# RWKV-7 inverse from blocks of 16 with pairs joined on TensorE, and sigmoids written with the hyperbolic tangent

## The chip, the cores and the metric

The kernel runs on one core of a Trainium2 chip, in one launch. The metric is the time of that launch on the device in microseconds (us). PE is TensorE, PEld its weight load, DVE is VectorE, ACT is ScalarE, POOL is GpSimd, and SP is SyncE, which issues all of this kernel's DMAs.

## The reference, cut to what matters

A decoder trunk of two layers works on 1024 tokens of width 1024: layer 0 is a latent attention (MLA) mixer, layer 1 an RWKV-7 mixer. Both have a memory cross-attention beside them and a gated output projection. The change lies in layer 1:

```python
def rwkv7_mixer(u_shift, mu, w0, w2, a0, a2, k_k, k_a, r_k, gn_w, gn_b):
    ...
    w = -jax.nn.softplus(-(w0 + jnp.tanh(wd) @ w2)) - 0.5
    decay = jnp.exp(-jnp.exp(w))
    a = jax.nn.sigmoid(a0 + ad @ a2)
    ...
    y = rwkv7_scan(r, decay, k, v, kk, a)      # 24 heads of 64 channels
def step(state, inp):                          # of rwkv7_scan, once for each token
    sa = einsum('bhvk,bhk->bhv', state, -kk_t)
    state = state * w_t + sa[..., None] * (kk_t * a_t) + v_t[..., None] * k_t
    return state, einsum('bhvk,bhk->bhv', state, r_t)
y = concatenate([mix, mem_out]) * jax.nn.silu(gate)
```

The decay of the reference equals exp(-exp(-0.5) * sigmoid(w0 + tanh(wd) @ w2)), so a sigmoid stands there too. The kernel computes the scan in chunks of 64 tokens. Within a chunk the tokens' feedback through `sa` is a strictly triangular 64x64 matrix A for each head, and the chunk needs the inverse of (I - A).

## The kernel before, in words

All products of weights are done in three passes of float32r (`mm3`, L162 to L164): high times high, high times low, low times high. A weight tile comes by DMA (`wr`, L152), ACT casts it to the high part (`wh`, L153), and in layer 1 DVE makes the low part (`wl`, L155). There are 4 buffers each of `wr`, `wh` and `wl`.

Layer 1 handles 24 items: 12 pairs of heads in each of 2 halves of 512 tokens; an item is 128 channels (2 heads) by 512 tokens (8 chunks), hence 16 systems of 64x64. An item goes through five stages, one in each of five successive steps of a software pipeline: `project` (r, k, v), `prep`, `invert`, `scan`, `norm`. In one step five items are in the works, one in each stage, and `interleave` writes their pieces in turns, with projections, memory heads and output projections as extra pieces. A scheduler then reorders each engine's instructions by its own account of durations and readiness; each engine and the SP queue run their list strictly in order. So an instruction that waits holds up everything behind it on its engine.

`prep` makes decays, keys and A: two low-rank products and sigmoids (`sig`, `a`, L998), three exponentials (L1038 to L1040), and the products masked into `AM` (L1090). It then writes the two diagonal 32x32 blocks of each system to DRAM (`sysd`, 16 DMAs of 8 KB, L1106) and copies the off-diagonal blocks A21 on ACT (L1109).

`invert` reads the blocks back with each one on 4 partitions (`As`, L1121; 32 blocks, 128 partitions), and a unit matrix split over those partitions (`U`, L1133), so that each partition solves for 8 columns. The back substitution is 31 pairs of DVE instructions, a product (`tmp`, L1139) and a sum (`U`, L1143) over up to 76 elements a partition. Eight transposes on PE (L1151) and four ACT copies (L1155) bring the solved blocks to the tile `inv` of 96 partitions (rows 0-31 A21, 32-63 and 64-95 the two inverted diagonal blocks). The off-diagonal block of the 64x64 inverse is U1 * A21 * U2: a DVE transpose (`X1`, in the trace X, L1159), four products on PE (L1174), four ACT copies (`M1`, L1183), four products (L1188), two ACT copies into `XT` (L1191). `XT` is the operand of the first dependent product of each chunk in `scan` (`c<-gm,XT`, L1221). The `scan` goes chunk by chunk between PE and DVE: L1217, `gm` (L1219), L1221, `SAV` (L1222), L1224, `S` (L1236).

On ACT, a table of functions is loaded (ACT_TABLE_LOAD) whenever the next function is not in the one that is active; in layer 1 the sigmoids (L998, and L864 in the gates) take turns with exponentials (L1037 to L1040, L304).

Of the kernel before, what the change touches and what calls it, by code (L numbers as in the profile page):

```python
# [71 lines left out]
class Build:  # L72
# [51 lines left out]


# [653 lines left out]
    def layer1(self, x1, first, second):  # L779

        nc, A, tc = self.nc, self.A, self.tc
        with ExitStack() as st:
# [19 lines left out]

            cen = tl([P, P], F32, "cen")
# [4 lines left out]
            for t in ARs + XTs + [U2]:  # L808
                nc.gpsimd.memset(t[:], 0.0)
# [169 lines left out]
    def prep(self, d, env):  # L979
# [14 lines left out]
        for j, (t, bias) in enumerate(((sig, PW0), (a, PA0))):  # L994
            ps = a_tile()
            mm(ps[:], wh[:, j * P : j * P + P], twa[j][:], start=True, stop=False)
            mm(ps[:], wl[:, j * P : j * P + P], twa[j][:], start=False, stop=True)
            ACT.activation(t[:], ps[:], AF.Sigmoid, bias=self.pc(bias + p))  # L998
# [98 lines left out]

        sysd = self.dram.tile([2, 16, 32, 32], F32, tag=f"sys{p % 2}", name=self.name("sysd"))
        inv = self.g([P, 16, 32], s="inv")
        A21 = inv[0:32]  # L1100
        for b in range(2):
            for i in range(4):
                src = AM[i][32 * b : 32 * b + 32, :, 0:128].rearrange("p c (h t) -> p c h t", h=2)
                dst = sysd[b, 4 * i : 4 * i + 4].rearrange("(c h) r t -> r c h t", h=2)
                for c in range(2):
                    nc.sync.dma_start(dst[:, c], src[:, c, :, 32 * b : 32 * b + 32])  # L1106
        for i in range(4):
            src = AM[i][0:32, :, 0:128].rearrange("p c (h t) -> p c h t", h=2)
            ACT.copy(A21[:, 4 * i : 4 * i + 4, :].rearrange("p (c h) t -> p c h t", h=2), src[:, :, :, 32:64])  # L1109
        d.update(f=f, SAV=SAV, BKT=BKT, AM=AM, bonus=bonus, inv=inv, sysd=sysd)  # L1110

    def invert(self, d, env):

        XT, U2, inv, sysd = (d[x] for x in ("XT", "U2", "inv", "sysd"))
# [5 lines left out]
        As = ip.tile([P, 32, 32], F32, tag="As", name=self.name("As"))  # L1120
        nc.sync.dma_start(  # L1121
            As[:].rearrange("p a b -> p (a b)"),
            sysd[:].rearrange("b s r t -> (b s) (r t)").unsqueeze(1).broadcast_to([32, 4, 1024]),
        )
        U = ip.tile([P, 32, 8], F32, tag="U", name=self.name("U"))
        tmp = ip.tile([P, 32, 8], F32, tag="tmp", name=self.name("tmp"))
        E = V
        if d["hf"] == 1:
            c0 = self.smp.tile([P, P], F32, tag="c0", bufs=2, name=self.name("c0"))
            nc.sync.dma_start(c0[:], self.carry[d["p"]][:])  # L1130
            ACT.activation(c0[:], c0[:], AF.Copy, scale=d["f"][:, 8:9])
            d["c0"] = c0[:]
        nc.sync.dma_start(U[:].rearrange("p a b -> p (a b)"), self.A["cst"][:, CU : CU + 256])  # L1133
        for u in range(31, 0, -1):
            if u % 4 == 0:
                yield
            i0 = u // 4
            n = 8 - i0
            E.tensor_tensor(  # L1139
                out=tmp[:, 0:u, 0:n], in0=As[:, 0:u, u : u + 1].broadcast_to([P, u, n]),  # L1140
                in1=U[:, u : u + 1, i0:8].broadcast_to([P, u, n]), op=ALU.mult,
            )
            E.tensor_tensor(out=U[:, 0:u, i0:8], in0=U[:, 0:u, i0:8], in1=tmp[:, 0:u, 0:n], op=ALU.add)  # L1143
        yield

        Uc = [inv[32:64], inv[64:96]]
        for ih in range(2):
            yield
            ps = b_tile()
            for i in range(4):  # L1150
                nc.tensor.transpose(ps[0:32, i * P : i * P + P], U[:, :, ih * 4 + i], self.ident)  # L1151
            for b in range(2):
                src = ps[0:32, :].rearrange("p (i s c) -> p i s c", i=4, c=4)[:, :, b * 16 : b * 16 + 16, :]
                dst = Uc[b][:, :, ih * 16 : ih * 16 + 16].rearrange("p s (i c) -> p i s c", c=4)
                ACT.copy(dst, src)  # L1155
# [143 lines left out]
def host_constants():  # L1299
# [79 lines left out]
```

## Time and profile before

| | |
|---|---|
| median of 3 runs | 2585.66 us (2582.15 to 2588.03) |
| the profiled execution's own time | 2576.96 us |
| its span, first to last instruction | 2575.1 us |
| mean granted TensorE clock | 0.991 |
| first and last `As` read (L1121) | 1088.2 and 2422.6 us after the span's start |
| DMA packets of the kernel | 165983, 231.46 MB |

The profiled execution is 8.7 us shorter than the median. The stretch from the first to the last `As` read, 1334 us, is called the pipeline stage below: it holds all 24 inversions but the end of the last.

### The profile page before, as it was taken

Reading aid. Unit: us, or ns where it says so; the run is one execution under the profiler, and the core shown is the slowest. Engines: PE = TensorE matmul, PEld = TensorE weight load, DVE = VectorE, ACT = ScalarE, POOL = GpSimd, SP = SyncE. Lnnn points to the kernel's source line nnn. Section 1 sums busy time; section 2 is a strip of 40 time slices with the busy share of each in tenths; the row PEclk is TensorE's granted clock in tenths of the full one; section 3 lists DMA queues with packets and bytes.
Section 4 is the critical chain, followed back from the end, with each engine's and each line's share of the span. In section 5 each row is a group of like instructions: output and inputs, shape, how many; then the busy total and the mean of one; then the engine's idle time right before and its main releaser. Section 6 shows DMA issues by size and latency. Waiting matters only on the chain.

```text
span 2575.1 us, 39906 instructions
## 1 busy us (share of the span) xinstructions
PE 2440.8 (95%) x13298; PEld 2004.1 (78%) x13298; DVE 1897.9 (74%) x5492; ACT 1374.2 (53%) x2971; POOL 367.7 (14%) x416
## 2 busy tenths in 40 slices
PE   7899999999999999999999999999999999999997
PEld 5687778888888788877777777777777777778775
DVE  6755334777777646698888888788888888786975
ACT  5444335555545434565665666666665655654542
POOL 4332222222211330010000000000000010000000
PEclk9999999999999999999999999999999999999998
DMA  4252222111112444422122222322222222232341
GB/s 161 86 172 89 80 82 76 47 59 50 56 60 70 142 158 145 139 79 74 61 65 74 77 74 83 103 78 78 70 77 73 69 85 94 94 99 96 107 146 68
DMA packets 165983, 231.46 MB, mean 90 GB/s; under 512 B 46096, under 2 KB 67984, under 8 KB 165776
## 3 DMA queue, kind: packets, MB, share of 16 engines
q1 hardware_dynamic: 165776, 228.90, 27.1%
q8 instruction: 105, 1.72, 0.3%
q14 instruction: 102, 0.84, 0.1%
HBM read 187.66 MB, written 37.49 MB: 87 GB/s over the span
## 4 chain that ended last, share of the span: by engine, by line
PE 64%; DVE 19%; ACT 5%; issue 5%; DMA 2%; SPq 0%; POOL 0%; POOLq 0%; DVEq 0%; ACTq 0%
PE mm L162 12%; PE mm L164 12%; PE mm L163 12%; PE a L1088 3%; DVE U L1143 2%; DVE tmp L1139 2%; PE pt L726 2%; DVE wl L155 2%; PE po L162 1%; PE po L163 1%; PE c L1221 1%; PE po L164 1%; PE c L1224 1%; DVE u L1019 1%; PE c L1215 1%
## 5 line engine op out<-in xcount | busy, mean ns | idle before, releaser
L153 ACT CAST wh<-wr 128x512 fp32r<-128x512 f32 (+3 forms) x500 | 298.7, 600 | 442.8 <-PE mm L163 362.8
L162 PE MATMUL mm<-xnh,wh 128*128 128x512 f32 x912 | 376.5, 413 | 0.6 <-DVE qml L134 0.4
L164 PE MATMUL mm<-xnh,wl 128*128 128x512 f32 x912 | 370.7, 407 | 1.1 <-DVE wl L155 1.1
L163 PE MATMUL mm<-xnl,wh 128*128 128x512 f32 x912 | 370.0, 406 | 0.0
L155 DVE TENSOR_TENSOR wl<-wr,wh 128x512 fp32r<-128x512 f32 (+2 forms) x352 | 238.5, 679 | 115.8 <-ACT wh L153 84.2
L155 POOL TENSOR_TENSOR wl<-wr,wh 128x512 fp32r<-128x512 f32 (+1 forms) x148 | 186.5, 1264 | 575.9 <-ACT wh L153 445.0
L162 PE MATMUL mm<-yh,wh 128*128 128x512 f32 x492 | 199.7, 406 | 5.9 <-DVE xr L391 5.9
L164 PE MATMUL mm<-yh,wl 128*128 128x512 f32 x492 | 196.3, 399 | 0.2 <-DVE wl L155 0.2
L162 PEld LDWEIGHTS mm<-xnh,wh 128*128 128x128 f32 x912 | 172.7, 190 | 30.4 <-issue 3.3
L164 PEld LDWEIGHTS mm<-xnh,wl 128*128 128x128 f32 x912 | 172.6, 189 | 29.9 <-DVE wl L155 1.3
L163 PE MATMUL mm<-yl,wh 128*128 128x512 f32 x492 | 195.4, 397 | 0.0
L163 PEld LDWEIGHTS mm<-xnl,wh 128*128 128x128 f32 x912 | 173.0, 190 | 26.1 <-issue 0.8
L162 PE MATMUL mm<-xh,wh 128*128 128x512 f32 x416 | 168.1, 405 | 7.7 <-ACT xh L440 7.7
L1235 ACT ACTIVATE sc<-S,f 128x128 f32<-128x128 f32 x168 | 67.4, 401 | 195.3 <-DVE S L1236 184.0
L1143 DVE TENSOR_TENSOR U<-U,tmp 128x60 f32<-128x60 f32 (+24 forms) x744 | 159.7, 215 | 13.5
L163 PE MATMUL mm<-xl,wh 128*128 128x512 f32 x416 | 167.5, 403 | 2.0 <-DVE xl L441 2.0
L164 PE MATMUL mm<-xh,wl 128*128 128x512 f32 x416 | 167.1, 402 | 0.0
L1139 DVE TENSOR_TENSOR tmp<-As,U 128x60 f32<-128x60 f32 (+24 forms) x744 | 157.1, 211 | 13.3 <-DMA U<-in_cst_dram 0.2
L992 POOL TENSOR_TENSOR w2l<-w,w2h 128x256 fp32r<-128x256 f32 x24 | 20.8, 865 | 897.9 <-ACT w2h L991 859.4
L304 ACT ACTIVATE p<-b,sm 128x512 f32<-128x512 f32 (+2 forms) x144 | 83.0, 580 | 117.5 <-DVE sm L301 78.2
L391 DVE TENSOR_TENSOR xr<-mm,xr 128x512 f32<-128x512 f32 x123 | 84.4, 688 | 77.2 <-PE mm L164 76.8
L162 PEld LDWEIGHTS mm<-yh,wh 128*128 128x128 f32 x492 | 92.8, 189 | 24.3 <-DVE xr L391 3.8
(362 smaller groups left out, 6300.0 us busy)
## 6 DMA issues: line engine op xcount, KB each, us to landing
wr<-in_wu_dram SPq DMA_DIRECT2D x292, 256.0 KB, 2.6
wr<-in_wo_dram SPq DMA_DIRECT2D x122, 256.0 KB, 2.6
yr<-y SPq DMA_DIRECT2D x60, 256.0 KB, 3.7
As<-sysd SPq DMA_DIRECT2D x24, 512.0 KB, 4.3
y<-y SPq DMA_DIRECT2D x32, 256.0 KB, 2.0
y<-sg SPq DMA_DIRECT2D x32, 256.0 KB, 2.1
g<-u SPq DMA_DIRECT2D x24, 256.0 KB, 2.5
gt<-g SPq DMA_DIRECT2D x24, 256.0 KB, 2.8
```

The source lines that it names most:

```text
L153: nc.scalar.copy(hi[:, :n], raw[:, :n])
L155: sub(lo[:, :n], raw[:, :n], hi[:, :n].bitcast(F32))
L162: mm(ps, a[0], b[0], start=start, stop=False)
L163: mm(ps, a[0], b[1], start=False, stop=False)
L164: mm(ps, a[1], b[0], start=False, stop=stop)
L304: nc.scalar.activation(p[:, :own], ps[:, :own], AF.Exp, bias=sm[:, 0:1], accum_out=sm[:, 2 + i : 3 + i])
L391: nc.vector.tensor_add(xs[m][:], ps[:], xs[m][:])
L726: nc.tensor.transpose(pt[:, o : o + P], src, self.ident)
L1088: mm(ps[:, j * 256 : j * 256 + 256], BK[c // 4][:, c % 4, :], AR[:, c, :], start=True, stop=True)
L1139: E.tensor_tensor(out=tmp[:, 0:u, 0:n], in0=As[:, 0:u, u : u + 1].broadcast_to([P, u, n]), in1=U[:, u : u + 1, i0:8].broadcast_to([P, u, n ...
L1143: E.tensor_tensor(out=U[:, 0:u, i0:8], in0=U[:, 0:u, i0:8], in1=tmp[:, 0:u, 0:n], op=ALU.add)
L1235: ACT.activation(sc[:], cur, AF.Copy, scale=fc)
```

## The change

It has two parts.

**The inverse.** The systems are written to DRAM whole (`sysd`, 8 DMAs of 64x2x64), and `invert` reads their four diagonal 16x16 blocks with each block on 2 partitions (`As`, 8 DMAs; 64 blocks, 128 partitions), and A21 (1 DMA in place of the four ACT copies). The back substitution is 15 pairs of DVE instructions of 8 to 120 elements a partition. The solved 16x16 blocks go to DRAM twice, as they are (`Wd`, 2 DMAs) and transposed in the row (`WT`, 2 DMAs, after the ACT copy `UT`). From there come the operands of the join (`W1T`; `W2`, in the rows W; and, from `sysd`, `N12`, in the rows N, 2 DMAs), and, in 4 DMAs, the 16x16 diagonal pieces of `inv`. The join of two 16-blocks to one 32-block is W1 * N12 * W2 for 32 pairs: four products on PE of 8 pairs each (new L1178), a mask on DVE (`Tb`, new L1183), four products on PE (new L1190), an ACT copy (`Ws`), a DMA to DRAM (`Wx`, new L1193) and two DMAs back to `inv` (new L1195). The eight transposes and the four copies L1155 are gone. From `inv` on (`X1`, new L1202; new L1217; `M1`, new L1226; new L1231; `XT`, new L1234; scan's new L1264) all is as before. `inv` is one tile for all items in place of a tile of the heap for each.

**The sigmoids.** sigmoid(x) becomes 0.5 * tanh(0.5 x) + 0.5: an ACTIVATE with Tanh and one with Copy, in `prep` (2 for each item) and in the gates (32 in all). The biases w0 and a0 are halved in place once.

```diff
+    def sigmoid(self, out, src, bias=None):
+        ACT.activation(out, src, AF.Tanh, scale=0.5, bias=0.0 if bias is None else bias)
+        ACT.activation(out, out, AF.Copy, scale=0.5, bias=0.5)
...
+            blk = tl([P, P], F32, "blk")
+            nc.sync.dma_start(blk[:], A["cst"][:, CU + P : CU + 256])
+            inv = tl([96, 16, 32], F32, "inv")
+            half = self.prm[:, PW0 : PW0 + 24]
+            nc.vector.tensor_scalar_mul(half, half, 0.5)
...
-                nc.scalar.activation(sg[:], ps[:], AF.Sigmoid)
+                self.sigmoid(sg[:], ps[:])
...
-            ACT.activation(t[:], ps[:], AF.Sigmoid, bias=self.pc(bias + p))
+            self.sigmoid(t[:], ps[:], env["half"][:, bias - PW0 + p : bias - PW0 + p + 1])
...
-        for b in range(2):
-            for i in range(4):
-                ...
-                for c in range(2):
-                    nc.sync.dma_start(dst[:, c], src[:, c, :, 32 * b : 32 * b + 32])
         for i in range(4):
-            ACT.copy(A21[:, 4 * i : 4 * i + 4, :].rearrange("p (c h) t -> p c h t", h=2), src[:, :, :, 32:64])
+            for c in range(2):
+                dst = sysd[4 * i + 2 * c : 4 * i + 2 * c + 2].rearrange("h r t -> r h t")
+                nc.sync.dma_start(dst, AM[i][0:64, c, 0:128].rearrange("p (h t) -> p h t", h=2))
...
-        nc.sync.dma_start(As..., sysd[:]...broadcast_to([32, 4, 1024]))
+        for half in range(2):
+            for i in range(4):
+                q = half * 64 + i % 2 * 32 + i // 2 * 16
+                nc.sync.dma_start(As[q : q + 16], sysd[:, 16 * i : 16 * i + 16, 16 * i : 16 * i + 16])
+        nc.sync.dma_start(A21, sysd[:, 0:32, 32:64].rearrange("s r t -> r s t"))
...
-        for u in range(31, 0, -1):
+        for u in range(15, 0, -1):
...
+        ACT.copy(UT[:].rearrange("p n r -> p r n"), U[:])
+            nc.sync.dma_start(Wd[:]...[:, :, cs], U[64 * half : 64 * half + 64])
+            nc.sync.dma_start(WT[:, cs, :], UT[64 * half : 64 * half + 32])
+        nc.sync.dma_start(W1T[:], WT[:].rearrange("q k m -> k q m"))
...
+        ps = b_tile()
+        for g in range(4):
+            mm(ps[:, g * P : g * P + P], N12[:, 8 * g : 8 * g + 8, :]..., W1T[:, 8 * g : 8 * g + 8, :]..., start=True, stop=True)
+        V.tensor_tensor(out=Tb[:], in0=ps..., in1=env["blk"]..., op=ALU.mult)
+        ps = b_tile()
+        for g in range(4):
+            mm(ps[:, g * 16 : g * 16 + 16], Tb[:, g, :], W2[:, g, :], start=True, stop=True)
+        ACT.copy(Ws[:].rearrange("p g n -> p (g n)"), ps[:, 0:64])
+        nc.sync.dma_start(Wx[:].rearrange("(g e) m n -> (e m) g n", e=8), Ws[:])
+        for j in range(2):
+            nc.sync.dma_start(inv[32 + 32 * j : 48 + 32 * j, :, 16:32], Wx[16 * j : 16 * j + 16]...)
-        for ih in range(2):
-            ...
-                nc.tensor.transpose(ps[0:32, i * P : i * P + P], U[:, :, ih * 4 + i], self.ident)
-            ...
-                ACT.copy(dst, src)
```

**How it stands in the engines' lists.** The scheduler's lists of the two kernels are the same up to the start of layer 1 but for the halving of the biases. The rows below are those of the fifth item (of 24) in the built programs; x4 is four equal rows, and a number behind a name tells buffers apart. First PE before, from the join of the 32-blocks (X is `X1`, the second M is `M1`) to the first product of scan that reads `XT`; the rows between the two pieces are all of one projection, and 22 rows lie between the last L1188 and L1221:

```order
L1174 MATMUL b_14048<-X_3043_14038,inv_13420 128x128 x4
L164 MATMUL mm_14120<-xnh_10265,wl_14110 128x512
L162 MATMUL mm_14120<-xnh_10292,wh_14109 128x512
L163 MATMUL mm_14120<-xnl_10293,wh_14109 128x512
L164 MATMUL mm_14120<-xnh_10292,wl_14110 128x512
L1188 MATMUL b_14058<-U_10130,M_3045_14053 32x128 x4
L162 MATMUL mm_14120<-xnh_10365,wh_14109 128x512
...
L1221 MATMUL c_14195<-gm_14193,XT_10128 128x128
```

PE now, from the new join of the 16-blocks to the same product; the rows left out are 24 of one projection:

```order
L1178 MATMUL b_13930<-W1T_13858,N_3055_13860 128x128 x2
L168 MATMUL mm_14064<-xnh_10474,wh_14059 128x512
L169 MATMUL mm_14064<-xnl_10475,wh_14059 128x512
L170 MATMUL mm_14064<-xnh_10474,wl_14060 128x512
L168 MATMUL mm_14064<-xnh_10519,wh_14059 128x512
L1190 MATMUL b_13962<-W_3056_13863,Tb_13935 128x16 x4
L169 MATMUL mm_14064<-xnl_10520,wh_14059 128x512
...
L1217 MATMUL b_13986<-X_3082_13976,inv 128x128 x4
L1231 MATMUL b_13996<-U_10134,M_3084_13991 32x128 x4
L1264 MATMUL c_14136<-gm_14134,XT_10132 128x128
```

Projection matmuls that stood between the steps of the old join now stand between L1190 and L1217, and none is left between L1217, L1231 and L1264. In 7 of the 24 items (the 1st, 3rd, 4th, 5th, 14th, 17th and 18th) no matmul stands between the last L1231 and L1264, and 0 to 2 between L1217 and L1231; in the other 17 there are 1 to 10 and 4. Before, 4 to 42 stood ahead of the use of `XT` and 4 to 12 between L1174 and L1188. Between L1178 and L1190 there are 4 in 11 items and 7 to 62 in the others; between L1190 and L1217 there are 26 to 38 in every item.

SP before, around the read of the same item's blocks:

```order
L1106 DMA sysd_13419<-AM_13354 32x2x32
L152 DMA wr_13941<-in_wu_dram 128x512
L1121 DMA As_13511<-sysd_13419 128x1x1024
L152 DMA wr_13947<-in_wu_dram 128x512
L1133 DMA U_13513<-in_cst_dram 128x256
L990 DMA w_3169_14635<-in_w2a_dram 128x256
```

SP now, from the read of the join's operands of that item to the loads behind it:

```order
L1159 DMA W1T_13858<-WT_13832 16x32x16
L1162 DMA N_3055_13860<-sysd_13378 16x16x16 x2
L1171 DMA inv<-Wd_13831 16x16x16 x3
L1112 DMA sysd_13937<-AM_13872 64x2x64 x2
L1193 DMA Wx_13833<-Ws_13967 128x4x16
L1139 DMA U_14031<-in_cst_dram 128x128
L158 DMA wr_14611<-in_wu_dram 128x512
L1130 DMA As_14021<-sysd_13937 16x16x16
L1195 DMA inv<-Wx_13833 16x16x16 x2
L1130 DMA As_14021<-sysd_13937 16x16x16 x7
L1131 DMA inv<-sysd_13937 32x16x32
L158 DMA wr_14617<-in_wu_dram 128x512
```

The queue has 361 rows more than before (1708 for 1347), and weight loads (`wr`) now stand behind DMAs that wait for PE's and ACT's part of the join.

More of the change, by code (lines that the diff above doesn't have):

```diff
@@ L807, in layer1 @@
             U2 = tl([P, 4, P], F32, "U2")
-            for t in ARs + XTs + [U2]:
+            for t in ARs + XTs + [U2, inv]:
                 nc.gpsimd.memset(t[:], 0.0)
@@ L1119, in invert @@
         V, G, ACT = nc.vector, nc.gpsimd, nc.scalar
[L1120 to L1127, printed above, removed]
+        As = ip.tile([P, 16, 16], F32, tag="As", name=self.name("As"))
@@ L1131, in invert @@
             ACT.activation(c0[:], c0[:], AF.Copy, scale=d["f"][:, 8:9])
             d["c0"] = c0[:]
-        nc.sync.dma_start(U[:].rearrange("p a b -> p (a b)"), self.A["cst"][:, CU : CU + 256])
-        for u in range(31, 0, -1):
-            if u % 4 == 0:
+        nc.sync.dma_start(U[:].rearrange("p a b -> p (a b)"), self.A["cst"][:, CU : CU + P])
+        for u in range(15, 0, -1):
+            if u % 2 == 0:
                 yield
[L1137 to L1141, printed above, removed]
-            )
-            E.tensor_tensor(out=U[:, 0:u, i0:8], in0=U[:, 0:u, i0:8], in1=tmp[:, 0:u, 0:n], op=ALU.add)
@@ L1144, in invert @@
-        yield
-        Uc = [inv[32:64], inv[64:96]]
-        for ih in range(2):
[L1148 to L1155, printed above, removed]
+            V.tensor_tensor(
+                out=tmp[:, 0:u], in0=As[:, 0:u, u : u + 1].broadcast_to([P, u, 8]),
+                in1=U[:, u : u + 1, :].broadcast_to([P, u, 8]), op=ALU.mult,
+            )
@@ new lines, in invert @@
+            V.tensor_tensor(out=U[:, 0:u], in0=U[:, 0:u], in1=tmp[:, 0:u], op=ALU.add)
+        UT = ip.tile([P, 8, 16], F32, tag="UT", name=self.name("UT"))
+        ACT.copy(UT[:].rearrange("p n r -> p r n"), U[:])
+        dt = lambda shape, n: self.dram.tile(shape, F32, tag=f"{n}{p % 2}", name=self.name(n))
+        Wd, WT, Wx = dt([2, 32, 16, 16], "Wd"), dt([32, 16, 16], "WT"), dt([32, 16, 16], "Wx")
+        for half in range(2):
+            cs = slice(8 * half, 8 * half + 8)
+            nc.sync.dma_start(Wd[:].rearrange("a q r n -> (a q) r n")[:, :, cs], U[64 * half : 64 * half + 64])
+            nc.sync.dma_start(WT[:, cs, :], UT[64 * half : 64 * half + 32])
@@ new lines, in invert @@
+        yield
+        W1T = self.g([16, 32, 16], s="W1T")
+        nc.sync.dma_start(W1T[:], WT[:].rearrange("q k m -> k q m"))
+        N12 = self.g([16, 32, 16], s="N12")
+        for j in range(2):
+            nc.sync.dma_start(
+                N12[:, 16 * j : 16 * j + 16, :],
+                sysd[:, 32 * j : 32 * j + 16, 32 * j + 16 : 32 * j + 32].rearrange("s k n -> k s n"),
+            )
+        W2 = ip.tile([P, 4, 16], F32, tag="W2", name=self.name("W2"))
+        nc.sync.dma_start(W2[:], Wd[1].rearrange("(g e) k n -> (e k) g n", e=8))
@@ new lines, in invert @@
+        for par in range(2):
+            for j in range(2):
+                r0, c0 = 32 + 32 * j + 16 * par, 16 * par
+                nc.sync.dma_start(
+                    inv[r0 : r0 + 16, :, c0 : c0 + 16], Wd[par, 16 * j : 16 * j + 16].rearrange("s r n -> r s n")
+                )
+        yield
+        ps = b_tile()
+        for g in range(4):
+            mm(
+                ps[:, g * P : g * P + P], N12[:, 8 * g : 8 * g + 8, :].rearrange("p q n -> p (q n)"),
+                W1T[:, 8 * g : 8 * g + 8, :].rearrange("p q m -> p (q m)"), start=True, stop=True,
+            )
@@ L1156, in invert @@
+        nc.sync.dma_start(Wx[:].rearrange("(g e) m n -> (e m) g n", e=8), Ws[:])
+        for j in range(2):
+            nc.sync.dma_start(
+                inv[32 + 32 * j : 48 + 32 * j, :, 16:32], Wx[16 * j : 16 * j + 16].rearrange("s r n -> r s n")
+            )
+        Uc = [inv[32:64], inv[64:96]]
         yield
```

33 lines of the change are left out of this document (20 added, 13 removed).

## Prediction

> **What bounds the kernel now.** I read the busy times first, then the pipeline stage alone, then the chain of waits there, then who makes PE wait.
>
> ```profile
> PE 2440.8 (95%) x13298; PEld 2004.1 (78%) x13298; DVE 1897.9 (74%) x5492; ACT 1374.2 (53%) x2971; POOL 367.7 (14%) x416
> ```
> ```profile
> 1088.00:2423.00 1335.00, 1268.78 (x7008) 1024.86 (x7007) 1118.03 (x3781) 807.25 (x1767) 99.26 (x112) 1.00 0.25 81
> ```
> ```profile
> by line: PE mm L162 9.4%; PE mm L164 9.3%; PE mm L163 9.1%; PE a L1088 5.7%; issue 3.6%; DVE U L1143 3.3%; DVE tmp L1139 3.2%; DVE wl L155 2.8%; PE c L1221 2.3%; PE c L1224 2.1%; DVE u L1019 2.0%; PE c L1215 2.0%; DVE L L1027 1.9%; PE y L12
> ```
>
> The second row is the pipeline stage: length, then PE, PEld, DVE, ACT and POOL busy. PE is at 95%, but DVE is at 84%, against 74% over the whole kernel. The third row is the chain of waits in that stage: besides projections, it runs through DVE, and the back substitution alone (U and tmp) holds 6.5%, 87 us of 1335. So PE is the first bound, with DVE close behind it: PE's list is held where a result of DVE or ACT is late.
>
> ```profile
> PEld c L1221 <- DVE gm L1219: 17.4, 30, 1.5
> PEld c L1215 <- DVE S L1236: 11.5, 35, 0.9
> PEld b L1151 <- ACT inv L1155: 11.4, 18, 0.8
> ```
> ```profile
> PEld b L1188 <- ACT M L1183: 10.2, 22, 0.6
> ```
>
> The four rows are waits of the weight loads in the stage (us in total, times, longest): all short, under 2 us, and many. The third goes away with the change.
>
> How much idle time there is to win depends on how PE's busy time is read. By PE's row the stage has 66 us in which PE does nothing, by the weight loads' row 310 us. The Trainium skill (Perfetto Trace Analysis, the note at its head) calls matmul busy time a bad metric, since matmuls are pipelined, and wants the weight loads' share: by that rule the larger figure holds, and a large gain (the third rival) is possible; by PE's row alone it could not pass 66 us. The trace bears the rule out in part: matmuls last 0.41 us in the groups and start every 0.23 us (rows below).
>
> **DVE's part.**
>
> ```profile
> L1143 DVE TENSOR_TENSOR U<-U,tmp 128x60 f32<-128x60 f32 (+24 forms) x713 | 153.3, 215 | 13.3
> L1139 DVE TENSOR_TENSOR tmp<-As,U 128x60 f32<-128x60 f32 (+24 forms) x713 | 150.2, 211 | 13.0 <-DMA U<-in_cst_dram 0.2
> L1090 DVE TENSOR_TENSOR AM<-a,cst 128x512 f32<-128x512 f32 x92 | 62.6, 682 | 2.6 <-PE a L1088 1.7 <-PE y L1227 0.4
> ```
> ```profile
> L1139 DVE TENSOR_TENSOR tmp<-As,U 128x60 f32<-128x60 f32 x69 | 14.9, 216 | 0.9
> ...
> L1139 DVE TENSOR_TENSOR tmp<-As,U 128x76 f32<-128x76 f32 x23 | 5.3, 231 | 0.3
> ...
> L1139 DVE TENSOR_TENSOR tmp<-As,U 128x8 f32<-128x8 f32 x23 | 4.1, 178 | 0.4
> ```
>
> An item's 62 instructions take (153.3 + 150.2) / 23 = 13.2 us. From 8 to 76 elements an instruction grows by 53 ns, so the new ones, 8 to 120 elements and 64 in the mean, take about 219 ns: 30 of them 6.6 us. The mask `Tb` has the form of L1090, 0.68 us. Together 7.3 us: 5.9 us less an item, 142 us less in all, 45% of the substitution. What reaches the end is what lies on the chain: 45% of 87 us, -39 us. Bounds: 0, if another path is as long at each place; and the whole 87 us, if the shorter substitution also lets DVE's other work arrive earlier. I take 39 because the chain is the nearest row to what decides.
>
> **PE's part.**
>
> ```profile
> L1151 PE MATMUL b<-cst,U 128*32 128x128 f32 x192 | 30.5, 275 | 5.3 <-ACT inv L1155 4.5 <-DVE U L1143 0.7
> L1174 PE MATMUL b<-X,inv 32*128 32x128 f32 x192 | 27.3, 281 | 3.5 <-DVE X L1159 2.2 <-ACT w2h L991 0.8
> ```
> ```profile
> L1006 PE MATMUL a<-cst,sq 128*128 128x2 f32 x192 | 23.5, 244 | 0.0
> ```
>
> A transpose leaves one record (8 an item, 192), a product of plain float32 two (4 an item in the code, 192 at L1174). The change takes 192 records away (30.5 us) and adds 8 products, 384 records: half like L1174 (few rows of K, 27.3 us), half like L1006 (16 columns out against 2, 23.5 us). So PE gets 50.8 - 30.5 = +20 us. Bounds: 0, if they fall into waits, and +51, if the transposes stood in waits. PE being the first bound, I take 20.
>
> **The waits of the join.** First the prices:
>
> ```profile
> 1538.69 0.23 PE mm L164
> 1538.92 0.23 PE mm L162
> ```
> ```profile
> L1183 ACT COPY M<-b 32x128 f32<-32x128 f32 x88 | 22.6, 257 | 26.1 <-PE b L1174 25.2
> ```
> ```profile
> L1191 ACT COPY XT<-b 32x256 f32<-32x256 f32 x44 | 15.6, 354 | 0.4
> ```
> ```profile
> L1159 DVE STREAM_TRANSPOSE X<-inv 32x512 f32<-32x512 f32 x24 | 16.8, 699 | 7.6 <-ACT inv L1155 7.1
> ```
> ```profile
> As<-sysd SPq DMA_DIRECT2D x24, 512.0 KB, 4.3
> ...
> sysd<-AM SPq DMA_DIRECT2D x384, 8.0 KB, 1.5
> ...
> U<-in_cst_dram SPq DMA_DIRECT2D x24, 128.0 KB, 2.3
> ...
> cr<-S SPq DMA_DIRECT2D x12, 64.0 KB, 1.8
> ```
>
> In the old list 4 projection matmuls (0.92 us) covered the copies `M1` (4 x 257 ns), and PE still waited 10.2 / 22 = 0.46 us: work of 1.03 us needs 1.38 us, 0.35 us being the two hand-overs. With that price:
> - In 7 items nothing covers `XT` now (2 x 354 ns + 0.35 = 1.06 us): +7 us. In the others 4 to 10 matmuls cover it, nearly.
> - `M1` loses its cover in 5 of these items (0.92 us each) and part of it in two: +6 us.
> - `Tb` (0.68 + 0.35 us) stands under 4 matmuls in 11 items: +1 us.
> - L1178 waits for the reads W1T and N, which land in about 2.3 us (U's row); the list gives them little cover in those 11 items: between 0 and 1 us each, I take 0.5, +5 us.
> - Between L1190 and L1217 the chain is Ws (0.26), the write Wx (1.8 by cr's row, as large in descriptors a partition), the second read (issued 0.33 later, 2.3) and X1 (0.70), with hand-overs 5.8 us; the least cover, 26 matmuls, is 5.9 us. I take 0: the cover is those projection matmuls, and if a leg is longer it is gone (second rival).
> - Gone: the waits of the transposes for L1155, -11 us.
>
> Together +8 us, between -11 (all covered) and +30 (N at 1 us, and Wx's chain 0.5 us late in every item).
>
> **ACT and SP.**
>
> ```profile
> L998 ACT ACT_TABLE_LOAD x22 | 28.2, 1283 | 0.4
> ```
> ```profile
> L1155 ACT COPY inv<-b 32x256 f32<-32x256 f32 x96 | 34.7, 362 | 12.6 <-PE b L1151 10.8
> ...
> L1109 ACT COPY inv<-AM 32x128 f32<-32x128 f32 x96 | 21.6, 293 | 0.3
> ...
> L1260 ACT ACTIVATE ys<-yT 128x512 f32<-128x512 f32 x24 | 15.0, 625 | 0.4 <-PE mm L164 0.3
> ```
> ```profile
> SPq L152 <- DVE wl L155: 309.3, 103, 16.3
> ```
> ```profile
> L152 SPq DMA_DIRECT2D wr<-in_wu_dram x292: 327/328/1048, 1.7 to 2333.8; - x146
> ```
>
> The built programs have 84 table loads before and 18 now: 66 x 1.283 = 85 us of ACT go. The second pass of a sigmoid (80 times, L1260's price) adds 50 us, UT and Ws about 16 us, and 56 us of copies go: ACT loses 75 of 807 us. The chain's row names no table load, and ACT is at 60%: I cost it at 0, between -10 us (the 10.2 us that PE waits for `M1` at L1188 go) and 0. The halving of the biases, the read of the mask and one more memset lie at the start of layer 1 under projections: 0.
>
> SP issues 361 DMAs more, at 0.33 us each 118 us. Its own wait for free `wr` buffers, 309 us in the stage, hides them. New is what stands behind a waiting one: behind Wx (waits for ACT, which waits for L1190) are U, a weight load and `As`; behind A21's read (waits for L1217) two weight loads. Two weight tiles are a whole projection; the 4 `wr` and 4 `wh` buffers cover such a hold of some us as long as SP is ahead. On DVE, X1 waits for the second read, with the next item's substitution and `wl` behind it.
>
> **Sum.** -39 + 20 + 8 = -11 us. The profiled execution (2576.96 us) lies 0.34% under the median of 2585.66, so I put the difference to the median: 2575 us, -0.4%. A measurement of this kernel tells about 0.2%, 5 us, from no change.
>
> **Rivals.**
> 1. *The relief does not reach the end* (slower). PE is at 95%, and in 7 items scan's first product now stands right behind XT. If the chain at the substitution has an equal one beside it, a third of the 39 us is left: -13 + 20 + 8 = +15, 2601 us; it decides once less than 28 us of relief arrive. For it: U and tmp have next to no wait of PE on them. Against it: DVE's 84%.
> 2. *A leg through DRAM is long* (slower). Wx is written in runs of 64 bytes, Wd in runs of 32. From sysd's 128-byte runs (1.5 us) nothing tells of it; As, the slowest read from sysd, takes 4.3 us. With 3 us for each of the two legs behind L1190 the chain is 7.7 us, 1.8 us over the least cover; with 0.7 us at L1178 that is 2.5 x 24 = 60 us, less what larger covers take (15): 2620 us. At 4.3 us it would be some 2680. It decides from legs of about 2.4 us. The Trainium skill (DMA: Bandwidth & Descriptors, Specifications) wants at least 512 bytes for line rate and says that below it the engine reads, modifies and writes: by that rule this rival gains. The runs of 128 bytes, which land sooner than cr's 512, speak against a large price.
> 3. *DVE was the true bound* (much faster). With the substitution's 39 us, the waits on gm and S (29 us) fall by half and ACT's 10 us come in: -39 - 15 - 10 + 28, 2550 us.
> 4. *No change*: 22 to 34 us of relief meet the 28 us of cost: 2580 to 2590, say 2585 us.
>
> **Chances.** The forecast (2561 to 2580) 0.32; rival 3 0.11; rival 4 0.20; rival 1 0.20; rival 2 0.17. Faster 0.43, same 0.20, slower 0.37. The range is 2545 to 2618: it leaves out half of rival 2 and the far end of rival 3, some 0.15. The forecast's own range is 2561 to 2580.
>
> **What the profile after will show.** Step right: DVE busy in the stage near 976 us, 720 instructions of tmp and U at about 219 ns; PE records 13490; ACT table loads 18. Wrong: the wait of L1178 or L1217 (X1) over 1 us an item, which is rival 2, or waits of L1264 on XT far over 1 us in 7 items and PE's chain share unchanged, which is rival 1. A weight load late for its cast (ACT's wh waiting for DMA wr), which no row shows now, would make it wrong in a way that no rival names.

## The result and the profile after

The changed kernel is slower: 2669.26 us (median of 4 runs, 2666.52 to 2673.79) against 2583.9 us for the kernel before beside it (4 runs, 2580.3 to 2588.03), a ratio of 1.0323 with a 95% interval of 1.0297 to 1.0349. Forecast were 2575 us and a range of 2545 to 2618 us. The profiled execution took 2673.79 us, its span is 2672.0 us.

First the busy times of the page, and the row of the pipeline stage (length, then PE, PEld, DVE, ACT and POOL busy, the granted clock, DMA share, GB/s), which now runs from 1088 to 2523 us, the last of the eight `As` reads of the last item:

```profile
PE 2526.0 (95%) x13490; PEld 2071.5 (78%) x13490; DVE 1799.1 (67%) x4749; ACT 1289.6 (48%) x2841; POOL 372.8 (14%) x417
```
```profile
1088.00:2523.00 1435.00, 1358.05 (x7236) 1096.23 (x7235) 1028.82 (x3078) 731.36 (x1652) 102.20 (x112) 0.96 0.30 77
```

DVE and ACT got their relief: DVE works 99 us less, ACT 85 us less, and the stage is still longer: from the first `As` read to the last item's first one it takes 1427 us against 1334. PE's shares of the span did not move (95% and 78%), so neither tells that anything is wrong. The last columns do: the granted clock of the stage fell from 1.00 to 0.96. Here is the page's clock row by slices:

```profile
PEclk8999999999999999998889999999999989999998
```

A drop of a tenth in a slice of 67 us hides what happens. In the stretch around the join of the fourth item, the windows (same columns as above) show it:

```profile
1300.00:1308.00 8.00, 8.00 (x41) 6.59 (x42) 2.55 (x5) 1.46 (x3) 0.00 (x0) 1.00 0.34 67
1308.00:1312.00 4.00, 2.85 (x19) 2.16 (x18) 3.02 (x10) 2.18 (x6) 0.00 (x0) 0.99 0.36 44
1312.00:1326.00 14.00, 11.48 (x39) 9.18 (x37) 9.32 (x44) 6.63 (x14) 1.06 (x1) 0.52 0.20 66
1326.00:1334.00 8.00, 7.19 (x35) 5.16 (x34) 6.22 (x13) 6.05 (x13) 3.39 (x3) 1.00 0.00 1
```

For 14 us the clock is at a half. The clock falls at 1311.9 us and is back at 1325.6. The timeline of PE shows what happens there (start, duration, engine, line, form; in brackets the idle time before and who ended it):

```profile
1308.64 0.39 PE L169 MATMUL mm<-xnl,wh 128*128 128x512 f32 x1
1308.87 0.39 PE L170 MATMUL mm<-xnh,wl 128*128 128x512 f32 x1
1309.18 1.15 PE L1217 MATMUL b<-X,inv 32*128 32x128 f32 x8
1311.49 1.55 PE L1231 MATMUL b<-U,M 128*32 128x128 f32 x8 [1.15 <-ACT M L1226]
1313.86 0.80 PE L1264 MATMUL c<-gm,XT 128*128 128x128 f32 x2 [0.82 <-ACT XT L1234]
1315.03 0.79 PE L1267 MATMUL c<-SAV,BKT 128*128 128x128 f32 x2 [0.37 <-DVE SAV L1265]
1315.62 0.63 PE L1271 MATMUL y<-SAV,AM 128*128 128x128 f32 x2
1316.65 1.87 PE L1017 MATMUL a<-cst,sq 128*128 128x2 f32 x8 [0.40 <-ACT sq L1014]
1319.45 0.80 PE L168 MATMUL mm<-xnh,wh 128*128 128x512 f32 x1 [0.93 <-DVE sg L876]
1320.04 0.63 PE L169 MATMUL mm<-xnl,wh 128*128 128x512 f32 x1
1320.47 0.63 PE L170 MATMUL mm<-xnh,wl 128*128 128x512 f32 x1
1320.89 0.63 PE L168 MATMUL mm<-xnh,wh 128*128 128x512 f32 x1
```

For 10.6 us there is no projection matmul between the products of the join, of scan and of `prep`; four of these, and the projection that ends the gap, wait for ACT or DVE, 0.4 to 1.15 us at a time. The first of the waits, 1.15 us for `M1`, is the only one ahead of the fall of the clock; the other four stand in the slow stretch. When the projections come back, they start every 0.43 us instead of every 0.23 us. So a wait here is paid twice: as the wait, and as half speed for what follows. The waits of PE in the stage at these five places (us in total, times, longest; the largest of all, L1053 for DVE's `rk`, is 15.6 us and was 11.5 before):

```profile
PE mm L168 <- DVE sg L876: 8.3, 8, 1.4
PE b L1231 <- ACT M L1226: 6.9, 7, 1.1
PE c L1267 <- DVE SAV L1265: 6.7, 13, 1.5
PE c L1264 <- ACT XT L1234: 6.0, 8, 0.8
PE a L1017 <- ACT sq L1014: 5.4, 10, 1.2
```

To add it up, I took from both traces each PE record's distance to the next one and compared it with the median distance of the same form at full clock. Where the clock was below 1, the distance counts as half speed up to the median divided by the clock, and the rest as idle. From 1088 us to the end of the span:

| | before | after | difference |
|---|---|---|---|
| work at full clock | 1269.3 | 1297.7 | +28 |
| half speed | 4.6 | 46.5 | +42 |
| idle while the clock was low | 0.7 | 34.4 | +34 |
| other idle | 202.8 | 195.7 | -7 |
| sum | 1477 | 1574 | +97 |

(The two profiled executions lie 97 us apart, the medians 85 us: the profile of before is a short one, that of after a long one.) The loss sits in the light steps of the pipeline, those without memory heads and output projections, in which four projections (96 matmuls) are all that PE has to fill in. Between successive `As` reads, the ten light steps (items 0-5 and 14-17) take 87.5 us more in sum than before, the other thirteen 5.6 us more. For items 2 to 5 a step took 48.8 us before (40.7 work, 8.1 idle) and takes 57.9 us now (43.1 work, 4.0 half speed, 3.4 idle at low clock, 7.4 other idle).

### The profile page after: what moved, and what is told of

Same layout as the page of the kernel before. It is cut to its first block, busy times and chain, and to the rows that moved or that the text cites. A ratio compares the mean times of both kernels' runs of the same rounds, so it can differ in the third digit from the quotient of the medians.

```text
span 2672.0 us, 40069 instructions
## 1 busy us (share of the span) xinstructions
PE 2526.0 (95%) x13490; PEld 2071.5 (78%) x13490; DVE 1799.1 (67%) x4749; ACT 1289.6 (48%) x2841; POOL 372.8 (14%) x417
## 4 chain that ended last, share of the span: by engine, by line
PE 76%; DVE 11%; ACT 5%; issue 2%; DMA 1%; SPq 0%; POOL 0%; DVEq 0%; POOLq 0%; ACTq 0%
PE mm L168 15%; PE mm L169 14%; PE mm L170 14%; PE a L1099 3%; PE c L1258 2%; PE pt L732 2%; PE c L1267 1%; PE po L168 1%; PE c L1264 1%; PE c L1260 1%; PE y L1270 1%; PE y L1271 1%; PE po L169 1%; PE po L170 1%; PE a L1017 1%
## 5 line engine op out<-in xcount | busy, mean ns | idle before, releaser
L168 PE MATMUL mm<-xnh,wh 128*128 128x512 f32 x912 | 385.3, 424 | 11.3 <-DVE sg L876 8.3
L169 PE MATMUL mm<-xnl,wh 128*128 128x512 f32 x912 | 378.0, 415 | 0.0
L170 PE MATMUL mm<-xnh,wl 128*128 128x512 f32 x912 | 376.1, 413 | 0.0
L168 PEld LDWEIGHTS mm<-xnh,wh 128*128 128x128 f32 x912 | 178.2, 196 | 42.6 <-DVE sg L876 9.0
L169 PEld LDWEIGHTS mm<-xnl,wh 128*128 128x128 f32 x912 | 178.5, 196 | 28.7 <-issue 1.2
L1308 POOL TENSOR_TENSOR yT<-yT,m 128x512 f32<-128x512 f32 x24 | 26.9, 1121 | 628.5 <-DVE n L205 211.8
L170 PEld LDWEIGHTS mm<-yh,wl 128*128 128x128 f32 x492 | 93.2, 189 | 18.3 <-issue 0.6
```

The source lines that it names most:

```text
L168: mm(ps, a[0], b[0], start=start, stop=False)
L169: mm(ps, a[0], b[1], start=False, stop=False)
L170: mm(ps, a[1], b[0], start=False, stop=stop)
L1308: G.tensor_tensor(out=yg, in0=yg, in1=wide(m[:, 0:8]), op=ALU.mult)
```

## The experiments

Below, "lost clock" is 1 minus the granted clock, summed over the span: 23.7 us before, 86.6 us after. "As to XT" is the time from the first `As` read to the end of `XT` in the light items 1-5 and 15-17, "slack" from there to the weight load of scan's first product that reads it, "light step" the distance of the `As` reads there; these three are means. The last four columns are worked out from the trace of one execution of each kernel.

| kernel | us | ratio to before (95%) | lost clock | As to XT | slack | light step |
|---|---|---|---|---|---|---|
| before | 2583.9 | 1 | 23.7 | 58.1 | 4.6 | 48.2 |
| changed | 2669.3 | 1.0323 (1.0297-1.0349) | 86.6 | 66.6 | 0.1 | 57.5 |
| 1 tanh alone | 2584.0 | 0.9996 (0.9982-1.0011) | 39.2 | 56.9 | 4.9 | 48.6 |
| 2 inverse alone | 2686.6 | 1.0393 (1.0368-1.0417) | 81.4 | 67.3 | 0.1 | 57.1 |
| 3 gate's bank | 2667.6 | 1.0318 (1.0295-1.0340) | 74.6 | 66.1 | 0.1 | 56.3 |
| 4 gate in one pass | 2670.7 | 1.0324 (1.0290-1.0358) | 72.7 | 65.4 | 0.1 | 56.8 |
| 5 join unread | 2637.7 | 1.0202 (1.0175-1.0229) | 50.3 | 62.4 | 0.1 | 55.1 |
| 6 two trips | 2738.9 | 1.0593 (1.0563-1.0623) | 133.0 | 76.8 | 0.2 | 56.7 |
| 7 early join | 2684.1 | 1.0383 (1.0340-1.0426) | 79.8 | 59.0 | 2.2 | 59.1 |
| 8 filler | 2655.3 | 1.0272 (1.0245-1.0299) | 47.1 | 64.7 | 0.1 | 55.5 |
| 9 one trip | 2625.0 | 1.0160 (1.0134-1.0185) | 47.4 | 66.6 | 0.4 | 51.1 |
| 10 half substitution | 2573.3 | 0.9963 (0.9946-0.9980) | 31.8 | 58.7 | 4.6 | 48.1 |
| 11 no join | 2549.2 | 0.9865 (0.9843-0.9888) | 28.4 | 55.8 | 5.2 | 47.0 |
| 12 later scan | 2676.0 | 1.0355 (1.0333-1.0377) | 71.2 | 64.2 | 0.1 | 54.7 |
| 13 thin filler | 2672.0 | 1.0318 (1.0292-1.0344) | 77.5 | 66.7 | 0.2 | 57.2 |

**Which part of the change?** Two theories: A, the gate's second ACT pass holds a projection's bank (the wait on `sg` above); B, the new join. Run 1 puts only the new sigmoids into before:

```diff
-                nc.scalar.activation(sg[:], ps[:], AF.Sigmoid)
+                self.sigmoid(sg[:], ps[:])
-            ACT.activation(t[:], ps[:], AF.Sigmoid, bias=self.pc(bias + p))
+            self.sigmoid(t[:], ps[:], env["half"][:, bias - PW0 + p : bias - PW0 + p + 1])
```

> Only the sigmoids are changed; the inverse is that of before. After the whole change 63 us more of lost clock (1 minus the granted clock, summed over the span: 86 against 23 us) stand in the profile, in stretches that begin where PE waits for XT, SAV, sq and the gate's sg one after the other. Theory A (the gate's second ACT pass holds a projection's bank, and that empties PE's list): this kernel alone is slower than before, 2610 to 2640 us, with 20 to 40 us more of lost clock and waits of L162-L164 on sg. Theory B (the new join uncovers XT and M1, and that empties the list): no slower than before, 2570 to 2590 us (ACT is rid of 66 table loads), lost clock near 23 us.

Run 2 is the changed kernel with those lines the other way round.

> Only the inverse is changed; the sigmoids are those of before, with their table loads. Theory A: near before, 2580 to 2610 us (the 20 us more of PE work of the prediction and little else). Theory B: nearly the whole loss, 2650 to 2680 us, with lost clock of 70 us or more and waits on XT and M1 in the items without cover.

Theory B holds and A falls: the sigmoids alone change nothing, the inverse alone loses 3.9%. With the new inverse the sigmoids even win 17 us (2686.6 to 2669.3). Runs 3 and 4, which test A directly, agree. Run 3 gives the gate's projection another bank:

```diff
-                    d["sg"] = gate(d["p"], d["hf"])
+                    free = i < 4 or 13 <= i <= 16
+                    d["sg"] = gate(d["p"], d["hf"], x_tile if free else self.mmt)
```

> The changed kernel, with the gate's projection in the eight items 0 to 3 and 13 to 16 in the PSUM bank x, which is free in those steps, so that it does not wait for the bank that the gate before it holds. These eight items carry some 36 us of the lost clock. Theory A: the waits of L168 on sg go there, and with them the half clock: 2630 to 2645 us. Theory B: the stretch stays empty, since the products after XT wait for XT all the same: 2660 to 2672 us, lost clock over 75 us.

Run 4 takes the second ACT pass off the gate:

```diff
-                self.sigmoid(sg[:], ps[:])
-                nc.vector.tensor_mul(sg[:], ps[:], sg[:])
+                nc.scalar.activation(sg[:], ps[:], AF.Tanh, scale=0.5)
+                nc.vector.scalar_tensor_tensor(sg[:], sg[:], 1.0, ps[:], ALU.add, ALU.mult)
...
-                self.split(hi[:], lo[:], t[:])
+                nc.scalar.activation(hi[:], t[:], AF.Copy, scale=0.5)
+                nc.vector.scalar_tensor_tensor(lo[:], t[:], 0.5, hi[:].bitcast(F32), ALU.mult, ALU.subtract)
```

> The changed kernel with the gate's second ACT pass gone: DVE makes (tanh + 1) times the projection in one instruction, and the factor 0.5 goes into the splitting of the output projection's operand. Theory A: the bank comes free 0.6 us or more earlier in each item, the stretches shorten and some no longer bring the clock down: 2640 to 2660 us. Theory B: 2665 to 2672 us.

Neither moves the time by more than its interval. In run 3 PE's waits on `sg` fell from 8.3 to 1.9 us, and others stand in its list of waits instead:

```profile
PE mm L168 <- DVE u L840: 13.6, 6, 4.2
...
PE c L1265 <- DVE gm L1263: 11.1, 9, 4.5
```

**Its lateness or its work?** The chain of an item behind its last U is long now: in the light items 2-5 it takes 24 us to the end of `XT` (UT, Wd and WT, the reads, L1178, `Tb`, L1190, `Ws`, Wx, the reads, X1, L1217, `M1`, L1231, `XT`) against 10 to 12 us before; the substitution ahead of it takes 31 us against 40, and starts 12 us after the first `As` read, not 6 to 9. Theory L: that lateness is the loss. Theory W: the join's instructions are. Run 5 keeps all instructions and lets nobody wait for the join:

```diff
+        spare = self.g([P, 16, 32], s="spare")
         for j in range(2):
             nc.sync.dma_start(
-                inv[32 + 32 * j : 48 + 32 * j, :, 16:32], Wx[16 * j : 16 * j + 16].rearrange("s r n -> r s n")
+                spare[32 + 32 * j : 48 + 32 * j, :, 16:32], Wx[16 * j : 16 * j + 16].rearrange("s r n -> r s n")
```

> The changed kernel with every instruction and DMA of the new join, but the two reads of Wx go to a spare tile, so that X1 and what follows don't wait for them; the joined block is left out of the inverse (it stays zero there). In the changed kernel's light steps an item takes some 25 us from its last U to its first L1264, against 9 to 12 before, and the substitution only got some 10 us shorter. Theory L (the join's chain of hand-overs and DMAs makes the item late, so that nothing is left to cover XT): with 8 us or more off the chain most of the loss goes, 2600 to 2630 us, lost clock under 50 us. Theory W (the join's work on PE, ACT and SP is the loss): no change, 2660 to 2675 us.

Run 11 leaves the join out, with the reads of its operands:

```diff
-        ps = b_tile()
-        for g in range(4):
-            mm(ps[:, g * P : g * P + P], N12..., W1T..., start=True, stop=True)
-        ... (Tb, the four products L1190, Ws, Wx and its reads)
```

> The changed kernel without the new join: L1178, Tb, L1190, Ws, Wx and the reads of their operands are left out, so the 16x16 blocks go through DRAM (Wd) into inv and straight on to X1. Against the kernel whose joined block nobody reads (2638 us) it has 368 PE records, 24 masks and 24 copies less. If the join's work on PE costs what its rows say (50 us), and the shorter chain covers XT again: 2560 to 2590 us. If only the chain matters and not the work: 2600 to 2640 us.

Neither theory holds alone. Against before, blocks of 16 without a join give -35 us, the join that nobody reads +88 us, and waiting for it +32 us; the sum is the 85 us. Of the 88 us (86 between the profiled executions), the account by distances gives 41 us to PE's work at full clock (run 11 has 1254.1 us of it, run 5 1294.9), 20 us to half speed, 11 us to idle at low clock and 13 us to other idle. Theory L's forecast for run 5 did not come, but run 5 does not refute it: it took away only half of the lateness. `XT` still ends 62.4 us behind `As` (55.8 in run 11, 66.6 in the changed kernel), in the items 2-5 it ends 22 us behind the last U, not 24, and nothing of the slack is back. So the 88 us hold lateness as well as work; and beside the join's instructions, run 5 has the copy `UT` and nine DMAs an item more than run 11.

Runs 6 and 9 add lateness alone, to the kernel before:

```diff
+        src96 = inv[32:96]
+        for n in range(2):        # run 9: range(1)
+            bd = self.dram.tile([64, 512], F32, tag=f"bd{n}{d['p'] % 2}", name=self.name("bd"))
+            nc.sync.dma_start(bd[:], src96.rearrange("p a b -> p (a b)"))
+            nx = self.g([P, 16, 32], s="inx")
+            nc.sync.dma_start(nx[32:96].rearrange("p a b -> p (a b)"), bd[:])
+            src96, Uc = nx[32:96], [nx[32:64], nx[64:96]]
```

> The kernel before, with nothing of the change, but the two inverted 32x32 blocks go to DRAM and back twice on their way to X1 (4 DMAs an item, some 10 us, no instruction on PE, DVE or ACT). Theory L: slow like the changed kernel or slower, 2640 to 2690 us, with lost clock of 60 us or more and waits for M and XT in the items without cover (13 of 24 in the built program). Theory W: 2580 to 2600 us, the DMAs being hidden.

> The kernel before with one trip of the two inverted blocks through DRAM instead of two (2 DMAs an item, some 5 us later). In the built program XT keeps 7 projection matmuls of cover in 17 items, where before had up to 35 and the two trips none in 13 items. If lateness costs only where the cover is used up: 2590 to 2625 us, far less than half of the 155 us of the two trips. If each us of lateness costs the same: about 2660 us.

Without one instruction more on PE, DVE or ACT, one trip costs 41 us and two cost 153 us by the ratios: lateness is dear by itself. It shows on DVE as well: the substitution waits 23.5 us (one trip) and 21.8 us (two) for the read of its unit matrix, 0.2 us before. PE itself waits for split weights at most 1.1 us in the stage. In the light items the first trip (8.5 us later) uses up the slack of 4.6 us, and the second meets none, which fits the bend. It is not all of it: of the steps' growth the ten light ones have 26 us with the first trip and 52 us more with the second, the other thirteen 17 and 54 us. Run 6's waits are those of the changed kernel, and above them stands that for the block itself:

```profile
PE b L1181 <- DVE X L1166: 40.1, 20, 8.1
...
PE c L1228 <- ACT XT L1198: 15.5, 15, 1.6
PE b L1195 <- ACT M L1190: 15.0, 15, 1.1
PE c L1231 <- DVE SAV L1229: 15.0, 25, 0.9
```

Run 9 also shows what lateness does not explain: with the same 66.6 us from `As` to `XT` as the changed kernel, its light step takes 51.1 us, not 57.5.

**Can the order repair it?** Run 7 moves the join forward in the item's step, run 12 moves scan back. Both leave all instructions as they are.

```diff
-            if u % 2 == 0:
+            if u == 8:
                 yield
...
-ST = (4, 18, 13, 11, 11)
+ST = (4, 18, 9, 11, 11)
```

> The changed kernel with the same instructions, but the substitution is written in 2 pieces in place of 8 and the stage gets 9 turns in place of 13, so that the join comes earlier in the item's step; in the built program 4 to 64 projection matmuls then cover M1 in all items and 2 to 50 cover XT in all but one. Theory L: the loss goes, 2570 to 2610 us, lost clock near before's 23 us, and the waits of PE on M, XT, sq and sg at the join go. Theory W: 2655 to 2675 us.

```diff
+                yield
                 yield from self.scan(d, env)
...
-ST = (4, 18, 13, 11, 11)
+ST = (4, 18, 13, 12, 11)
```

> The changed kernel, same instructions, but scan's first chunk is written one turn later (12 turns in place of 11, the first one empty), so that in the built program 4 projection matmuls cover M1, 6 cover XT and 3 cover SAV in most light items, where the changed kernel has none in seven. If the missing cover at the join is the loss: 2605 to 2645 us with lost clock under 50 us. If a light step simply has too few projection matmuls for its chains, and cover given to the join is missing in scan (as in the early join): 2655 to 2685 us.

Neither helps, though in run 7 M1 and XT are covered; by the medians run 7 is 15 us slower than the changed kernel, but the intervals of the two ratios overlap. The timeline of PE in run 7 shows where the cover was taken from:

```profile
1289.79 0.49 PE L1264 MATMUL c<-gm,XT 128*128 128x128 f32 x2 [0.38 <-DVE gm L1262]
1290.65 0.49 PE L1267 MATMUL c<-SAV,BKT 128*128 128x128 f32 x2 [0.38 <-DVE SAV L1265]
1291.65 0.80 PE L1258 MATMUL c<-SAV,AM 128*128 128x128 f32 x2 [0.51 <-DVE S L1279]
1292.24 0.63 PE L1260 MATMUL c<-S,AR 128*128 128x128 f32 x2
1293.26 0.80 PE L1264 MATMUL c<-gm,XT 128*128 128x128 f32 x2 [0.38 <-DVE gm L1262]
```

Now scan's chunks stand alone, and the clock halves there (windows of run 7, columns as above):

```profile
1286.00:1290.00 4.00, 2.80 (x16) 1.87 (x15) 1.81 (x6) 1.50 (x4) 0.00 (x0) 1.00 0.33 33
1290.00:1308.00 18.00, 15.84 (x54) 12.52 (x54) 4.51 (x11) 5.22 (x15) 0.00 (x0) 0.53 0.19 32
1308.00:1314.00 6.00, 6.00 (x35) 5.28 (x35) 2.88 (x7) 1.04 (x4) 0.00 (x0) 0.98 0.26 71
```

The projection matmuls of a light step are a fixed stock. The early join spends them on itself, and scan's own chain, which had them before, went bare.

**Is the halved clock a cause of its own?** Run 8 gives PE more work: 18 matmuls of 384 columns whose results nobody uses, in the empty places of ten items. Run 13 has the same matmuls with 2 columns.

```diff
+        def fill(ps, n, behind):
+            with self.tc.issue_after(behind.ins):
+                for _ in range(n):
+                    mm(ps[:, P:T], twa[0][:, 0:P], twa[1][:, 0 : T - P], start=True, stop=True)
...
+                    fill(pa, 6, d["m1"])     # behind L1217
+                    fill(pa, 5, d["m2"])     # behind L1231
+                    fill(py, 3, mpa)         # behind L1264
+                    fill(py, 4, my)          # behind L1271
```

> The changed kernel with MORE work on PE: in the ten items 0-4, 13, 15-17 and 19, 18 matmuls of 384 columns whose results nobody uses stand in PE's list in the empty places of the join (6 behind L1217, 5 behind L1231, 3 behind L1264, 4 behind L1271), some 3 us an item or 30 us in all, about as long as PE waits there. If the halved clock is a cost of its own (half of the loss by the rows: some 43 us of matmuls at half speed), the fillers hold the clock up and the kernel gets faster with more work: 2635 to 2660 us, lost clock under 60 us. If the low clock only goes along with the waits, nothing is won: 2668 to 2700 us.

> The control of the filler: the changed kernel with the same 18 unused matmuls in the same places of the same ten items, but of 2 columns in place of 384, so that they add next to no activity on PE; PE's list around the join stays that of the changed kernel (M1 and XT without cover in seven of these items). If the filler won because its matmuls kept PE active and so the clock up: nothing is won here, 2663 to 2678 us, lost clock over 75 us. If it won by the places in the list that it pinned: 2650 to 2660 us.

With some 30 us of useless work the kernel got 14 us faster, with the thin matmuls in the same places it did not. The runs of the two do not overlap (2653.6 to 2657.4 and 2667.6 to 2676.2 us); their ratios' intervals just touch. Beside the thin matmuls the kernel before took 2589.0 us, beside the filler 2583.7; by the ratios 12 us lie between the two. The windows of one stretch, of the changed kernel, of run 8 and of run 13 in this order:

```profile
1300.00:1326.00 26.00, 22.33 (x94) 17.93 (x95) 14.89 (x58) 10.26 (x22) 1.06 (x1) 0.74 0.27 63
```
```profile
1300.00:1326.00 26.00, 24.60 (x120) 19.68 (x118) 17.79 (x64) 14.54 (x31) 3.26 (x2) 0.91 0.25 58
```
```profile
1300.00:1326.00 26.00, 24.67 (x112) 21.09 (x111) 14.53 (x60) 11.87 (x27) 1.06 (x1) 0.74 0.26 59
```

The granted clock is 0.74, 0.91 and 0.74. By the account of distances, run 8 has 35 us more work than the changed kernel, 28 us less of half speed, 27 us less of idle at low clock and 3 us more of other idle: 17 to 18 us less, as the spans show (2672.0 and 2654.4 us). So the halving is a cost beside the waits; it follows them, and how much PE works in them decides whether it comes and how long it lasts.

**What is DVE's relief worth?** Run 10 is the kernel before with every second step of the substitution left out:

```diff
-        for u in range(31, 0, -1):
+        for u in range(30, 0, -2):
```

> The kernel before with every second step of the back substitution left out (30 instructions an item of up to 60 elements in place of 62), nothing else: the relief of DVE by itself, some 6.8 us an item or 160 us in all. By the prediction's term (45 to 50% of the 87 us that U and tmp hold on the chain) it gives -39 us or more: 2535 to 2550 us. If DVE's time is not what PE waits for, no more than 10 us: 2573 to 2588 us.

```profile
PE 2444.5 (95%) x13298; PEld 2007.6 (78%) x13298; DVE 1782.9 (69%) x4724; ACT 1374.1 (53%) x2971; POOL 368.8 (14%) x416
```

DVE works 115 us less, the kernel gains 10 us (5 to 14 by the interval). `As` to `XT` did not get shorter at all (58.7 against 58.1 us in the light items), although the substitution did: in the items 2-5 it takes 16.2 us from its first product to its last U, not 40.0. The rows of the fourth item, two of before and two of run 10, show where this went (its `As` read is issued at 1217.80 and at 1216.62 us):

```profile
1265.18 0.17 DVE L1143 TENSOR_TENSOR U<-U,tmp 128x8 f32<-128x8 f32 x1
1267.96 0.60 PE L1151 MATMUL b<-cst,U 128*32 128x128 f32 x4
```
```profile
1241.41 0.16 DVE L1143 TENSOR_TENSOR U<-U,tmp 128x16 f32<-128x16 f32 x1
1267.82 0.60 PE L1151 MATMUL b<-cst,U 128*32 128x128 f32 x4
```

Counted from the `As` read, the last U comes 23 us earlier, and the transposes that read it start no sooner (51.2 us behind the read, 50.2 before): PE's list has them behind projection matmuls. In run 10 PE never waits for U there; before, PE and its weight loads waited 2.4 us for it in all.

## Why the prediction was wrong, step by step

Of the sum -39 + 20 + 8, the first term failed most (10 us in run 10), and one term is missing: the clock at half speed, +42 us.

- **The relief, -39 us: mis-sized by a factor of four.** The step "what reaches the end is what lies on the chain: 45% of 87 us" failed; run 10 has a like relief and gains 10 us. A share of the chain of waits tells who came last, not what the end would gain: the path beside U and tmp is PE's own list, which reaches the transposes no sooner when U is ready 23 us earlier. Rival 1 said so, for a third of the relief; in the kernel before it was a quarter.
- **PE's part, +20 us: right in kind, too small.** L1178 holds 31.3 us and L1190 23.2 us, less 30.5 us of transposes, +24 us; all PE work at full clock grew by 28 us.

```profile
L1178 PE MATMUL b<-W1T,N 16*128 16x128 f32 x192 | 31.3, 290 | 0.0
...
L1190 PE MATMUL b<-W,Tb 128*128 128x16 f32 x192 | 23.2, 253 | 0.0
```

- **The waits of the join, +8 us: the named ones were right, the sum was wrong.** M1 was priced at +6 and XT at +7; PE's rows above have 6.9 and 6.0 (on the weight loads' rows, from which the price came, M1 went from 10.2 to 15.4). L1178 was priced at +5 and waits 0.0. The upper bound of +30 does not come out of its terms, which give +26. What failed is that each wait was priced alone and at full clock. The seven places where XT had no cover were seen, but not that SAV, sq and sg then wait in the same bare stretch, nor that the clock halves there: +42 us of half speed, which neither the sum nor a rival holds, and +27 us of idle where the sum had -31 (-39 of relief, +8 of waits).
- **Wx's chain, 0 us:** what waits for it costs 32 us (run 5 against the changed kernel). The legs were as short as assumed:

```profile
Wd<-U SPq DMA_DIRECT2D x48, 32.0 KB, 2.6
...
Wx<-Ws SPq DMA_DIRECT2D x24, 32.0 KB, 1.8
inv<-Wx SPq DMA_DIRECT2D x48, 16.0 KB, 2.1
```

  So rival 2 falls in its mechanism (a long leg), though lateness behind the legs is part of the loss. The cover of 26 matmuls was there (PE waits 2.8 us for X1 in the stage), but it was taken from the places behind it, and `XT` came 8.5 us later behind `As` than before in the light items, where only 4.6 us of slack stood. The rule of the Trainium skill that spoke for rival 2 (DMA: Bandwidth & Descriptors, Specifications: below 512 bytes the engine reads, modifies and writes) shows here at most for Wd's runs of 32 bytes: 2.6 us, against 1.8 us for Wx's 64-byte runs and 1.9 us for `sysd`'s, which are of 256 bytes now, all in DMAs of 32 KB.
- **ACT's part, 0 us: right by itself.** 66 table loads less and 80 second passes more changed nothing in before (run 1). Together with the new inverse they gain 17 us, which was not foreseen.
- **SP's part, 0 us: right in the main.** The queue waits 73 us for `Ws` and 47 us for L1217, as foreseen. ACT's casts wait 5.6 us for the reads `wr` of `wu` over the whole span (5.5 before), and in the stage 10.8 us more that the trace puts down to other DMAs of the queue (before, 0.7 us for all DMAs). PE waited 1.0 us for a cast there.
- **Rival 3 (DVE was the true bound) falls** with run 10.
- **The signs.** DVE busy in the stage is 1029 us, not 976, in a longer stage: the 317 us of tmp and U rows overlap other DVE rows, only 214 us of them stand alone, so DVE was relieved of 99 us and not of 142; tmp and U take (86.8 + 81.5) / 720 = 234 ns, not 219; PE records are 13490 and table loads 18, as forecast. The sign for rival 1, waits of L1264 on XT "far over 1 us", did not appear (0.8 us at most on PE's row, 1.3 on the weight loads'), and yet the kernel lost more than rival 1 said.

What stays open: at which activity the clock halves, and how the 88 us of the unread join divide between its work, its DMAs, the lateness that is left in run 5 and the other order of PE's list that comes with it. No kernel that does the whole computation was faster than before; run 1 is level with it.

## What to carry to other kernels

Where PE runs through the waits of several dependent chains, count the independent matmuls that are left to cover them, step by step: a new chain with little work of its own costs what it takes from the others, and in runs 7 and 12 a better place for it in the list only moved the bare stretch. Price waits that follow one another as one stretch, and add the half speed after it; the granted clock in windows of a few us shows it, the busy share does not. Test a relief by leaving work out before costing it by the chain's shares, and look where the instruction that reads its result stands in the other engine's list.

## What the runs showed of the hardware that was not expected

- The clock went to 0.50 without a long pause of PE: in the stretch shown, no idle time was over 1.15 us, and the fall came right behind that one. The Trainium skill (TensorE: Matmul & The Clock Gate, HAM oscillation) gives as the abstract rule that no idle gap may pass some 3.4 us. This trace differs: of the 14 falls in the stage, one follows an idle time of 3.47 us, the others shorter ones or, once, none over 0.15 us. The passage of the Trainium skill on a second failure mode (same title, A second HAM failure mode: psum-queue depth-cycling), short idles between groups of matmuls, is nearer, though four of the falls here have a single such wait, of 1.15 us, in the 3.4 us ahead.
- The low stretches, but for the one that runs into the end of the kernel, cost 1.7 us of clock or a multiple of it (1.71, 3.41, 5.12 and 6.83 us), that is halves of 3.41 us. The Trainium skill (TensorE: Matmul & The Clock Gate, Part 1, What's actually happening) states a window of 3413 ns and a clock of either all or half; the trace agrees.
- More work can be faster: 180 matmuls whose results nobody uses took 14 us off the time, the same matmuls with 2 columns nothing.
- PE's rows covered 45 to 71% of the 3.4 us ahead of 11 of the 14 falls in the stage (4, 35 and 100% ahead of the others). In the kernel before, two such stretches with 53% passed without one, so the share of busy time does not tell when the clock falls.
